# Modulation by weighted sums on VectorE, ScalarE and GpSimd with a matmul of ones, in place of split matmuls

## The chip, the cores and the metric

The kernel runs on one core of a Trainium2 chip. The metric is the device time of one execution in microseconds. One core has five engines with queues of their own that run in order: TensorE (PE in the profile; its weight loads are PEld), VectorE (DVE), ScalarE (ACT), GpSimd (POOL) and SyncE (SP, which issues most DMAs). On-chip memory is SBUF with 128 partitions, and matmuls write to PSUM banks.

## The reference

Two blocks of a small transformer follow each other on 512 tokens x and 256 context tokens ctx, with 1024 features. The first block has two layers (called AB and CD in the kernel). Each is modulated by a conditioning vector, one for x and one for ctx:

```python
mod = silu(c) @ mod_w[l] + mod_b[l]          # [3072], for c of x and of ctx
h, gate = adaln(x, mod)                      # rmsnorm(x) * (1 + scale) + shift
... AB: MLA and GQA attention over [ctx | x];  CD: windowed attention and a short convolution
x = x + gate * (mixed @ w_out)
```

So each layer needs six vectors (shift, scale, gate for x and ctx) of 1024 numbers each, which come out of 2 x 1024 times 1024 x 3072 products. The second block has an even and an odd layer without this modulation.

## The kernel before, in words

All products are made from fp32 operands that are split into a high and a low part in fp32r: `mm3` (lines 236 to 240) issues three matmuls, high x high (L238), high x low (L239) and low x high (L240). `weights` (L210) loads a chunk of weights in pieces of 512 KB into a ring of 3 raw slots (`rawp`), casts each half on ScalarE (L229) and subtracts on VectorE, or in some filler work on GpSimd, for the low part (L232). `split` (L141) does the same for activations (L143, L144). `rstd` (L135) is a root by a power on GpSimd (L138), which each normalisation waits for. Temporaries of up to 2 KB per partition come from `T4`, a ring with the tag `t2` of 5 slots in the stage that the change touches; `sc` holds silu(c) as two columns per feature block, and `sc4` its split.

The modulation of the first layer's shift and scale is made in `start` by `mod_first` and is not touched. The rest comes by chunks of 256 columns. `mod_rows` (L328) loads a chunk, splits it, and multiplies it with `sc4` as the stationary operand of 4 columns: 16 matmuls of 4x256 (L338 for the high part, L339 for the low part) into one F bank, which VectorE copies out as 4 rows (L340), with the bias as a fifth row. `mod_cols` (L343) turns rows into columns by two matmuls with a 5x2 selector (L348). `mods` (L742) does both for eight chunks of layer 1 (the kernel counts layers from 0). For the gates, `gate_rows` (L353) spills the five rows to DRAM and `gate_sum` (L359) loads them again, sums them by a matmul with the selector (L364) and spills two rows.

The tile framework puts the instructions of each engine in an order of its own, worked out by a timeline model from the order in which the code is written, from priorities and from the slots that rings have; engines then wait for each other by semaphores. In `run` (L1424) the AB layer begins with the latents (`ab_lat`, L747: two column chunks, in each three pairs of token tiles, which are projected, normalised, transposed and split), then `mla_proj` for four head groups (`proj(0)` to `proj(3)`), the queries `ab_q` and gates `ab_gates`. `mods` is written in between: chunks 0, 1 between the two halves of `ab_lat`, 2, 3 after it, 4 to 7 between the head groups, and the gate of layer 0 at the end. The first attention scores (L469) follow. In the CD layer, `rest` (L1626) is a generator whose units are spread over the attention items by `pace(items, ru, 21)`; `gate_rows` for layer 1 are four of these units, and `gate_sum` is one.

## Time and profile before

| what | value |
|---|---|
| median of 3 runs | 1550.33 us (1548.44 to 1553.42) |
| profiled execution, first to last instruction | 1546.3 us |
| what lies around it against the median | 4.0 us |
| mean granted TensorE clock | 0.990 of full speed |
| busy: PE, PEld | 96%, 89% of the span |
| busy: DVE, ACT, POOL | 67%, 55%, 35% |
| moved by DMA | 168.2 MB, 109 GB/s in the mean |

The busy shares are means over the whole program. The change touches two stretches: the AB layer's projections, from some 73 us to the first attention score at 254 us, and the CD layer's attention with its fillers, from some 640 to 780 us. What a saved microsecond is worth there has to be read from windows over these stretches, from the waits in them, and from the order of the queues. Matmuls overlap: what one costs is the distance between the starts of two, not the duration of one.

### The profile page before, as it was taken

The page shows a single profiled execution, that of the slowest core. Times are in us where ns is not written, and L with a number is a line of the kernel's source. Part 1 is how long each engine was busy: PE and PEld are TensorE (multiplying, and loading weights), DVE is VectorE, ACT ScalarE, POOL GpSimd, SP SyncE. Part 2 cuts the span into 40 slices and gives each one's busy share as a digit, 9 for nine tenths or more (in the row PEclk, how much of TensorE's full clock was granted, in tenths as well). Part 3 has the DMA queues.
Part 4 walks back from the last instruction along what each step waited for, and adds up shares of the span by engine and source line. Part 5 has one row for each costly group of instructions (what it writes and reads, how often), then busy time and mean ns, then how long its engine had stood idle before and what let it go on. Part 6 is the DMA issues. An engine that isn't in the chain of part 4 may idle for free.

```text
span 1546.3 us, 28606 instructions
## 1 busy us (share of the span) xinstructions
PE 1486.4 (96%) x10760; PEld 1373.0 (89%) x10760; DVE 1036.5 (67%) x2121; ACT 846.5 (55%) x1759; POOL 546.9 (35%) x652
## 2 busy tenths in 40 slices
PE   6899999989999999999999999999999999999998
PEld 3799788877998999888889889998899999998998
DVE  6777887889886477777755458986544465565444
ACT  6545555689996154565643446557433544455322
POOL 1533533567674033232421434444201334443000
PEclk8999999999999999999999999999999999999999
DMA  8344564121221332322234222124334321223423
GB/s 304 121 128 120 183 203 162 45 103 33 63 70 31 146 121 71 101 96 86 93 115 145 80 96 82 66 86 137 116 103 143 119 94 57 82 69 132 148 90 110
DMA packets 60685, 168.20 MB, mean 109 GB/s; under 512 B 9890, under 2 KB 18530, under 8 KB 60546
## 3 DMA queue, kind: packets, MB, share of 16 engines
q1 hardware_dynamic: 54768, 163.52, 31.8%
q10 hardware_dynamic: 5778, 2.84, 0.7%
q8 instruction: 85, 1.39, 0.4%
q14 instruction: 54, 0.44, 0.1%
HBM read 144.06 MB, written 22.28 MB: 108 GB/s over the span
## 4 chain that ended last, share of the span: by engine, by line
PE 79%; DVE 8%; DMA 5%; ACT 3%; issue 2%; POOL 2%; SPq 0%; ACTq 0%; DVEq 0%; POOLq 0%
PE A L240 17%; PE A L238 17%; PE A L239 17%; PE B L524 3%; PE F L238 3%; PE F L239 3%; PE F L240 3%; PE F L595 2%; PE B L238 2%; PE B L239 2%; PE B L240 2%; DVE wl L232 1%; PE B L996 1%; PE B L388 1%; PE B L1168 1%
## 5 line engine op out<-in xcount | busy, mean ns | idle before, releaser
L229 ACT CAST wh<-raw 128x512 fp32r<-128x512 f32 (+1 forms) x388 | 232.4, 616 | 237.8 <-PE A L240 166.9
L232 DVE TENSOR_TENSOR wl<-raw,wh 128x512 fp32r<-128x512 f32 (+1 forms) x320 | 233.4, 744 | 93.9 <-ACT wh L229 90.7
L481 POOL TENSOR_SCALAR P<-P,s 128x768 f32<-128x768 f32 (+3 forms) x192 | 152.8, 801 | 176.4 <-DVE s L1264 33.4
L144 DVE TENSOR_TENSOR PTl<-B,PTh 128x512 fp32r<-128x512 f32 (+2 forms) x208 | 127.9, 633 | 47.7 <-ACT PTh L143 35.0
L232 POOL TENSOR_TENSOR wl<-raw,wh 128x512 fp32r<-128x512 f32 x68 | 90.9, 1338 | 158.3 <-ACT wh L229 132.0
L138 POOL TENSOR_TENSOR s8f<-s8f,mhalf 128x4 f32<-128x4 f32 (+2 forms) x53 | 61.5, 1161 | 227.3 <-DVE s8f L137 119.7
L238 PE MATMUL A<-wh,mh 128*128 128x256 f32 x480 | 136.5, 285 | 2.9 <-ACT mh L143 2.9
L143 ACT CAST PTh<-B 128x512 fp32r<-128x512 f32 (+2 forms) x208 | 108.2, 545 | 53.8 <-PE B L524 27.1
L239 PE MATMUL A<-wl,mh 128*128 128x256 f32 x480 | 136.0, 284 | 0.0
L240 PE MATMUL A<-wh,g 128*128 128x256 f32 x408 | 115.7, 285 | 1.2 <-DVE g L144 1.2
L240 PE MATMUL A<-wh,h2l 128*128 128x256 f32 x384 | 108.7, 286 | 2.5 <-DVE h2l L408 2.5
L238 PE MATMUL A<-wh,h4h 128*128 128x256 f32 x384 | 109.5, 286 | 1.0 <-ACT h4h L407 0.8
L240 PE MATMUL A<-wh,h4l 128*128 128x256 f32 x384 | 108.7, 285 | 0.5 <-DVE h4l L408 0.5
L238 PE MATMUL A<-wh,h2h 128*128 128x256 f32 x384 | 108.9, 284 | 0.3 <-ACT h2h L407 0.3
L239 PE MATMUL A<-wl,h4h 128*128 128x256 f32 x384 | 108.7, 284 | 0.0
L239 PE MATMUL A<-wl,h2h 128*128 128x256 f32 x384 | 108.6, 283 | 0.0
L238 PEld LDWEIGHTS A<-wh,mh 128*128 128x128 f32 x480 | 91.9, 192 | 4.3 <-ACT mh L143 3.3
L239 PEld LDWEIGHTS A<-wl,mh 128*128 128x128 f32 x480 | 92.0, 192 | 0.1
L524 PE MATMUL B<-ident,P 128*128 128x128 f32 x592 | 86.2, 274 | 4.5 <-DVE PTl L144 2.4
L240 PEld LDWEIGHTS A<-wh,g 128*128 128x128 f32 x408 | 78.0, 192 | 1.7 <-DVE g L144 1.7
L490 ACT ACTIVATE P<-A,s 128x768 f32<-128x768 f32 (+1 forms) x96 | 73.2, 766 | 7.4 <-DVE s L488 4.7
L524 PEld LDWEIGHTS B<-ident,P 128*128 128x128 f32 x592 | 67.5, 141 | 9.2 <-POOL P L481 2.5
(515 smaller groups left out, 4914.8 us busy)
## 6 DMA issues: line engine op xcount, KB each, us to landing
raw<-mod_w SPq DMA_DIRECT2D x32, 512.0 KB
raw<-even_w SPq DMA_DIRECT2D x32, 512.0 KB
raw<-odd_w SPq DMA_DIRECT2D x32, 512.0 KB
raw<-cd_w SPq DMA_DIRECT2D x26, 512.0 KB
mraw<-mod_w SPq DMA_DIRECT2D x16, 512.0 KB
raw<-w_ple_gate SPq DMA_DIRECT2D x16, 512.0 KB
raw<-ab_wg SPq DMA_DIRECT2D x8, 512.0 KB
raw<-ab_wo SPq DMA_DIRECT2D x8, 512.0 KB
```

The costliest lines, as they stand in the source:

```text
L138: self.nc.gpsimd.tensor_tensor(out=ms, in0=ms, in1=self.mhalf[:, 0:n], op=ALU.pow)
L143: self.nc.scalar.copy(out=hi, in_=src)
L144: self.nc.vector.tensor_tensor(out=lo, in0=src, in1=f32(hi), op=ALU.subtract)
L229: nc.scalar.copy(out=hi, in_=r)
L232: eng.tensor_tensor(out=lo, in0=r, in1=f32(hi), op=ALU.subtract)
L238: mm(out=out, lhsT=xh, rhs=wh, start=start, stop=False)
L239: mm(out=out, lhsT=xh, rhs=wl, start=False, stop=False)
L240: mm(out=out, lhsT=xl, rhs=wh, start=False, stop=stop)
L481: self.nc.gpsimd.tensor_scalar(out=P, in0=P, scalar1=s, scalar2=0.0, op0=ALU.mult, op1=ALU.add)
L490: nc.scalar.activation(out=P[:, u, :], in_=S[:, u, :], func=AF.Exp, bias=m[:, u:u + 1], scale=1.0, accum_out=s[:, u:u + 1])
L524: nc.tensor.transpose(out=pt[:, j, u, :], in_=b, identity=self.ident)
L595: nc.tensor.matmul(out=O, lhsT=vst(e, j), rhs=pts[j // 2][w][:, j % 2], start=w + j == 0, stop=w == 1 and j == nk - 1)
```

## The change

For the gate of layer 0 (two parts of 512 columns), for shift and scale of layer 1 (four parts) and for the gate of layer 1 (two parts, x alone), the product is no longer made by matmuls over split weights. `acc_part` loads a part by four transfers of 512 KB into the raw ring and goes over the eight feature blocks: VectorE multiplies the raw [128, 512] weights with the column of silu(c) for x and adds to an accumulator `ax`; for ctx, ScalarE multiplies into a temporary of `T4` and GpSimd adds it to an accumulator `ac`. The sum over the 128 partitions is then a matmul in fp32 with a column of ones: `acc_cols` makes 8 of them per part, 128x1 each, for columns; `acc_gate` makes one row of 512 per gate and spills it. The accumulators are halves of gate buffers (`gT[4]` to `gT[7]`), two pairs in turn. The spill of five rows, `mod_rows`, `gate_rows`, `gate_sum` and `mods` go; biases come as inputs of another layout. In CD the counted units become 22 with `pace` still at 21.

```diff
-            self.ab_lat(X, L, latg, lambda: self.mods(0, 1))
-            self.mods(2, 3)
+            gs2 = [[gT[b + i][:, 0:512] for i in range(2)] for b in (4, 6)]
+            am = self.acc_mods([gs2[j] for j in (0, 1, 0, 1, 1, 1)])
...
+            self.ab_lat(X, L, latg, lambda: acc(5))
+            acc(5)
             proj(0)
+            acc(5)
             T["q"] = {0: self.ab_q(X, gp, T, 0)}
+            acc(5)
             proj(1)
-            self.mods(4, 5)
+            acc(5)
             self.ab_gates(X, 2, keep(4))
+            acc(5)
             proj(2)
-            self.mods(6, 7)
             self.ab_gates(X, 3, keep(6))
             proj(3)
-            self.gate_rows(0, range(4))
-            self.gate_sum(0)
             self.ab_gates(X, 0, spill(0))
...
-                    for h in (2 * g, 2 * g + 1):
-                        self.gate_rows(1, (h,))
+                    a3 = self.acc_part(6 + g, (self.tl(cp, [128, 512], "ax", 1), None))
+                    for h in range(2):
+                        next(a3)
+                        next(a3)
                         yield
+                    next(a3, None)
+                    self.acc_gate(1, g)
+                    yield
...
-                self.gate_sum(1)
-                yield
```

The new functions (here and in the rows of the new order below, line numbers are the changed kernel's; `acc(5)` is one whole part):

```python
    def acc_part(self, j, into):
        nc = self.nc
        self.macc = ax, ac = into
        for k in range(8):
            if k % 2 == 0:
                raw = self.tl(self.rawp, [128, 2, 512], "raw")
                nc.sync.dma_start(out=raw, in_=self.I["mod_r"][j][:, k:k + 2, :])
            r = raw[:, k % 2, :]
            if k == 0:
                nc.vector.tensor_scalar(out=ax, in0=r, scalar1=self.sc[:, k, 0:1], scalar2=None, op0=ALU.mult)
            else:
                nc.vector.scalar_tensor_tensor(out=ax, in0=r, scalar=self.sc[:, k, 0:1], in1=ax, op0=ALU.mult, op1=ALU.add)
            if ac is not None:
                if k == 0:
                    nc.scalar.activation(out=ac, in_=r, func=AF.Copy, scale=self.sc[:, k, 1:2])
                else:
                    t = self.T4([128, 512])
                    nc.scalar.activation(out=t, in_=r, func=AF.Copy, scale=self.sc[:, k, 1:2])
                    nc.gpsimd.tensor_tensor(out=ac, in0=ac, in1=t, op=ALU.add)
            if k % 2:
                yield

    def acc_cols(self, j):
        nc = self.nc
        p = self.B()
        for e, a in enumerate(self.macc):
            for b in range(4):
                nc.tensor.matmul(out=p[:, 2 * b + e:2 * b + e + 1], lhsT=a[:, 128 * b:128 * b + 128], rhs=self.ones)
        nc.vector.tensor_tensor(out=self.modT[1][:, 4 * j:4 * j + 4, :], in0=p[:, 0:8].rearrange("p (b e) -> p b e", e=2),
                                in1=self.mbias[:, 4 * j:4 * j + 4].unsqueeze(2).to_broadcast([128, 4, 2]), op=ALU.add)

    def acc_gate(self, layer, h, bank="F"):
        nc = self.nc
        for e, a in enumerate(self.macc):
            if a is not None:
                cs = slice(512 * h, 512 * h + 512)
                r, p = self.T4([1, 512]), self.B(bank)
                nc.scalar.dma_start(out=r, in_=self.I["mod_bg"][layer:layer + 1, cs])
                nc.tensor.matmul(out=p[0:1, :], lhsT=self.ones, rhs=a)
                nc.vector.tensor_tensor(out=r, in0=p[0:1, :], in1=r, op=ALU.add)
                nc.sync.dma_start(out=self.gsum_d[layer][e:e + 1, cs], in_=r)
```

**First place: GpSimd's queue at the latents.** The code of `ab_lat` before and in the change; L138, now L143, is the power of a normalisation (`s_...`), and each pair of token tiles of the latents has one of 128x2. Before:

```order
L138 TENSOR_TENSOR s_238_1039<-s_238_1039,mhalf 128x2
L138 TENSOR_TENSOR s_243_1105<-s_243_1105,mhalf 128x2
L138 TENSOR_TENSOR s_248_1171<-s_248_1171,mhalf 128x2
L138 TENSOR_TENSOR s_289_1345<-s_289_1345,mhalf 128x2
L138 TENSOR_TENSOR s_294_1411<-s_294_1411,mhalf 128x2
L138 TENSOR_TENSOR s_299_1477<-s_299_1477,mhalf 128x2
L138 TENSOR_TENSOR s8f_1599<-s8f_1599,mhalf 128x4
```

Now:

```order
L143 TENSOR_TENSOR s_238_1042<-s_238_1042,mhalf 128x2
L143 TENSOR_TENSOR s_243_1108<-s_243_1108,mhalf 128x2
L363 TENSOR_TENSOR g_20_116<-g_20_116,t_251_1192 128x512
L143 TENSOR_TENSOR s_248_1174<-s_248_1174,mhalf 128x2
L363 TENSOR_TENSOR g_20_116<-g_20_116,t_253_1198 128x512
L363 TENSOR_TENSOR g_20_116<-g_20_116,t_254_1202 128x512
L363 TENSOR_TENSOR g_20_116<-g_20_116,t_256_1208 128x512
L363 TENSOR_TENSOR g_20_116<-g_20_116,t_257_1212 128x512
L363 TENSOR_TENSOR g_20_116<-g_20_116,t_259_1218 128x512
L363 TENSOR_TENSOR g_20_116<-g_20_116,t_260_1222 128x512
L143 TENSOR_TENSOR s_278_1310<-s_278_1310,mhalf 128x2
L143 TENSOR_TENSOR s_283_1376<-s_283_1376,mhalf 128x2
```

Behind the second pair's power, the first part's seven additions into `g_20` stand around the third pair's power (`s_248`) and ahead of those of the second chunk.

**Second place: ScalarE's queue at the same point.** L755, now L782, squares a pair of latents, L143, now L148, casts the transposed latents, and L229, now L234, casts weights. Before, with the modulation's weights `wh` among the latents' work, up to the first cast for the next chunk that follows there:

```order
L229 CAST wh_1274<-raw_1272 128x512
L229 CAST wh_1278<-raw_1272 128x512
L229 CAST wh_1284<-raw_1282 128x512
L279 COPY t_246_1167<-A_1118 128x512
L229 CAST wh_1288<-raw_1282 128x512
L143 CAST lTh_949<-B_1045 128x2x256
L755 ACTIVATE t_247_1169<-t_246_1167 128x512
L333 DMA t_260_1204<-mod_b 1x256
L143 CAST lTh_949<-B_1111 128x2x256
L333 DMA t_273_1248<-mod_b 1x256
L143 CAST lTh_949<-B_1177 128x2x256
L229 CAST wh_1492<-raw_1490 128x512
```

Now:

```order
L148 CAST lTh_952<-B_1048 128x2x256
L782 ACTIVATE t_247_1172<-t_246_1170 128x512
L362 ACTIVATE t_251_1192<-raw_1187,sc 128x512
L362 ACTIVATE t_253_1198<-raw_1195,sc 128x512
L148 CAST lTh_952<-B_1114 128x2x256
L362 ACTIVATE t_254_1202<-raw_1195,sc 128x512
L362 ACTIVATE t_256_1208<-raw_1205,sc 128x512
L362 ACTIVATE t_257_1212<-raw_1205,sc 128x512
L362 ACTIVATE t_259_1218<-raw_1215,sc 128x512
L148 CAST lTh_952<-B_1180 128x2x256
L362 ACTIVATE t_260_1222<-raw_1215,sc 128x512
L234 CAST wh_1239<-raw_1237 128x512
```

Where casts of modulation weights stood, the scaled copies (L362) stand, each into a temporary `t_...` that an addition on GpSimd frees; behind them stands `wh_1239`, the first cast of the second chunk of latent weights.

**Third place: TensorE's queue in the head projections.** F is the bank of the modulation's columns, B those of the head projections. Before, the end of a modulation chunk:

```order
L238 MATMUL A_2275<-hTh_122,wh_2216 128x512
L239 MATMUL A_2275<-hTl_123,wh_2216 128x512
L240 MATMUL A_2275<-hTh_122,wl_2217 128x512
L348 MATMUL F_2152<-sel_79,t_435_2132 128x2 x2
L238 MATMUL B_2029<-whf_2025,lTh_949 128x256
L239 MATMUL B_2029<-wlf_2026,lTh_949 128x256
L240 MATMUL B_2029<-whf_2025,lTl_950 128x256
```

Now, where shift and scale's second part ends (L373 are the matmuls with ones):

```order
L243 MATMUL B_2459<-whf_2367,lTh_952 128x384
L244 MATMUL B_2459<-wlf_2368,lTh_952 128x384
L245 MATMUL B_2459<-whf_2367,lTl_953 128x384
L373 MATMUL F_2034<-ones,g_22_118 128x1 x4
L243 MATMUL B_2483<-whf_2363,lTh_952 128x384
L244 MATMUL B_2483<-wlf_2364,lTh_952 128x384
L245 MATMUL B_2483<-whf_2363,lTl_953 128x384
```

The matmuls with ones of `g_22`, the accumulator for ctx, stand in the middle of the projections of `proj(2)`. On GpSimd, the seven additions into that accumulator are ordered like this now, from the second to the last (`mk_2044`, L877, are the keys of `proj(1)`, and `s8f` normalisations):

```order
L363 TENSOR_TENSOR g_22_118<-g_22_118,t_401_2007 128x512
L363 TENSOR_TENSOR g_22_118<-g_22_118,t_402_2011 128x512
L143 TENSOR_TENSOR s8f_2096<-s8f_2096,mhalf 128x4
L877 TENSOR_TENSOR mk_2044<-t2f_2065,mgk_959 128x4x64
L363 TENSOR_TENSOR g_22_118<-g_22_118,t_404_2017 128x512
L877 TENSOR_TENSOR mk_2044<-t2f_2092,mgk_959 128x4x64
L363 TENSOR_TENSOR g_22_118<-g_22_118,t_405_2021 128x512
L143 TENSOR_TENSOR s8f_2123<-s8f_2123,mhalf 128x4
L363 TENSOR_TENSOR g_22_118<-g_22_118,t_407_2027 128x512
L877 TENSOR_TENSOR mk_2044<-t2f_2119,mgk_959 128x4x64
L143 TENSOR_TENSOR s8f_2382<-s8f_2382,mhalf 128x4
L363 TENSOR_TENSOR g_22_118<-g_22_118,t_408_2031 128x512
```

The additions alternate with the powers and key products of `proj(1)`, and the accumulator is whole only with the last of these rows, behind three key products and three powers.

## Rows read from the trace of the kernel before

**Rows 1.** Page, span and busy time of each engine.

```profile
span 1546.3 us, 28606 instructions
...
PE 1486.4 (96%) x10760; PEld 1373.0 (89%) x10760; DVE 1036.5 (67%) x2121; ACT 846.5 (55%) x1759; POOL 546.9 (35%) x652
```

**Rows 2.** Windows (start:end, wall; busy PE, PEld, DVE, ACT, POOL; clock; DMA; GB/s).

```profile
100.00:240.00 140.00, 136.54 (x955) 120.51 (x954) 110.27 (x259) 75.51 (x152) 52.10 (x49) 1.00 0.54 172
640.00:780.00 140.00, 139.68 (x820) 118.40 (x819) 103.87 (x238) 88.21 (x200) 44.30 (x69) 1.00 0.27 88
```

**Rows 3.** Waits of PE, 60 to 255 us (the longest: total, times, longest).

```profile
PE A L240 <- DVE wl L232: 1.5, 1, 1.5
```

**Rows 4.** Waits of PE, 640 to 780 us (the only one).

```profile
PE F L238 <- DVE t2f L340: 0.3, 1, 0.3
```

**Rows 5.** Instructions of line L338 (duration min/median/max, first and last start).

```profile
L338 PE MATMUL F<-wh,sc x128: 275/276/362, 73.7 to 732.3; 128*4 128x256 f32 x128
```

**Rows 6.** Timeline of PE (start us, us, instruction) in the AB layer's projections.

```profile
103.27 0.60 PE L348 MATMUL F<-sel,t 5*128 5x2 f32 x4
103.80 0.39 PE L239 MATMUL A<-wl,hTh 128*128 128x256 f32 x1
...
106.61 0.28 PE L339 MATMUL F<-wl,sc 128*4 128x256 f32 x1
...
108.24 0.28 PE L339 MATMUL F<-wl,sc 128*4 128x256 f32 x1
...
235.72 1.01 PE L364 MATMUL F<-t,sel 5*2 5x512 f32 x2
```

**Rows 7.** Groups by form, 60 to 255 us (busy us, mean ns | idle before, releaser).

```profile
L232 DVE TENSOR_TENSOR wl<-raw,wh 128x512 fp32r<-128x512 f32 x76 | 53.2, 724 | 4.7 <-ACT wh L229 4.6
...
L229 ACT CAST wh<-raw 128x512 fp32r<-128x512 f32 x76 | 44.1, 619 | 26.6 <-PE F L338 6.7 <-DMA raw<-mod_w 5.1 <-DMA raw<-ab_wg 4.6
...
L138 POOL TENSOR_TENSOR s8f<-s8f,mhalf 128x4 f32<-128x4 f32 x24 | 27.9, 1165 | 40.2 <-DVE s8f L137 39.9
...
L850 POOL TENSOR_TENSOR mk<-t2f,mgk 128x256 f32<-128x256 f32 x12 | 10.1, 839 | 12.2 <-DVE t2f L848 6.5 <-DMA qkv_d<-mk 5.7
...
L138 POOL TENSOR_TENSOR s<-s,mhalf 128x2 f32<-128x2 f32 x6 | 5.5, 913 | 26.5 <-DVE s L137 26.4
...
L163 DVE SCALAR_TENSOR_TENSOR g<-t,A 128x512 f32<-128x512 f32 x4 | 2.7, 674 | 0.0
```

**Rows 8.** Page, group of GpSimd's subtractions.

```profile
L232 POOL TENSOR_TENSOR wl<-raw,wh 128x512 fp32r<-128x512 f32 x68 | 90.9, 1338 | 158.3 <-ACT wh L229 132.0
```

**Rows 9.** Timeline of POOL, two products of 128x512.

```profile
152.55 1.54 POOL L191 TENSOR_TENSOR t<-t,TQ 128x512 f32<-128x512 f32 x1
...
164.33 1.66 POOL L191 TENSOR_TENSOR t<-t,TQ 128x512 f32<-128x512 f32 x1
```

**Rows 10.** Timeline of DVE at the same times.

```profile
152.85 1.78 DVE L193 TENSOR_TENSOR q<-t,TQ 128x512 f32<-128x512 f32 x1
...
164.15 0.69 DVE L193 TENSOR_TENSOR q<-t,TQ 128x512 f32<-128x512 f32 x1
```

**Rows 11.** Timeline of SP, the two issues of a chunk's loads.

```profile
110.75 9.58 SPq L222 DMA_DIRECT2D raw<-ab_wq  x2
```

**Rows 12.** Timeline of ACT, the cast that waits for the second of these loads.

```profile
123.77 1.14 ACT L229 CAST wh<-raw 128x512 fp32r<-128x512 f32 x2 [0.58 <-DMA raw<-ab_wq]
```

**Rows 13.** Timeline of PE, the matmuls behind a pause.

```profile
76.58 0.39 PE L238 MATMUL A<-wh,hTh 128*128 128x256 f32 x1 [1.35 <-ACT pk L702]
...
80.21 0.41 PE L238 MATMUL A<-wh,hTh 128*128 128x256 f32 x1
```

**Rows 14.** Timeline of PE, end of the first latent chunk; first attention score.

```profile
97.56 0.28 PE L240 MATMUL A<-wh,hTl 128*128 128x256 f32 x1
...
254.49 0.36 PE L469 MATMUL A<-kA,qs 128*128 128x256 f32 x1 [0.92 <-DVE t L163]
```

More of the change, by code (lines that the diff above doesn't have):

```diff
@@ L108, in setup @@
         self.dram = ent(self.pool("dram", space=DRAM))
-        self.grow_d, self.gsum_d = ([self.dram.tile([n, 1024], F32, name=f"g{n}row{l}_d") for l in range(2)] for n in (5, 2))
+        self.gsum_d = [self.dram.tile([2, 1024], F32, name=f"grow{l}_d") for l in range(2)]
         self.rot_d = [self.dram.tile([128, 4, 2, n], F32, name=f"rot{n}_d") for n in (16, 32)]
@@ L115, in setup @@
         nc.vector.memset(self.mhalf, -0.5)
+        self.ones = c.tile([128, 1], F32, name="ones")
+        nc.vector.memset(self.ones, 1.0)
         self.sel2 = c.tile([5, 2], F32, name="sel2")
@@ L121, in setup @@
         nc.scalar.dma_start(out=self.ng, in_=I["norm_g_2"])
+        self.mbias = c.tile([128, 16], F32, name="mbias")
+        nc.scalar.dma_start(out=self.mbias, in_=I["mod_bc"])
+        nc.vector.tensor_scalar(out=self.mbias[:, 8:16], in0=self.mbias[:, 8:16], scalar1=1.0, scalar2=None, op0=ALU.add)
         self.modT = [c.tile([128, 16, 2], F32, name=f"modT{l}") for l in range(2)]
@@ L326, in mod_first @@
         return rows, self.sel2
-    def mod_rows(self, layer, ch):
-        nc = self.nc
-        W = self.weights(self.I["mod_w"][layer, ch])
-        rows = self.T4([5, 256])
-        nc.scalar.dma_start(out=rows[4:5, :], in_=self.I["mod_b"][layer:layer + 1, 256 * ch:256 * ch + 256])
-        p = self.B()
-        for k0, hi, lo in W:
-            for k in range(hi.shape[1]):
-                kk = k0 + k
-                nc.tensor.matmul(out=p[0:4, 0:256], lhsT=self.sc4[:, kk, :], rhs=hi[:, k, :], start=kk == 0, stop=False)
-                nc.tensor.matmul(out=p[0:4, 0:256], lhsT=self.sc4[:, kk, :], rhs=lo[:, k, :], start=False, stop=kk == 7)
-        nc.vector.tensor_copy(out=rows[0:4, :], in_=p[0:4, 0:256])
-        return rows, self.sel2
     def mod_cols(self, layer, ch, rs):
@@ L351, in mod_cols @@
                                      op0=ALU.mult, op1=ALU.add)
-    def gate_rows(self, layer, chs):
-        for h in chs:
-            rows, _ = self.mod_rows(layer, 8 + h)
-            self.nc.sync.dma_start(out=self.grow_d[layer][:, 256 * h:256 * h + 256], in_=rows)
-    def gate_sum(self, layer, bank="F"):
-        for h in (0, 512):
-            rows, r, p = self.T4([5, 512]), self.T4([2, 512]), self.B(bank)
-            self.nc.sync.dma_start(out=rows, in_=self.grow_d[layer][:, h:h + 512])
-            self.nc.tensor.matmul(out=p[0:2, :], lhsT=self.sel2, rhs=rows)
-            self.nc.scalar.copy(out=r, in_=p[0:2, :])
-            self.nc.sync.dma_start(out=self.gsum_d[layer][:, h:h + 512], in_=r)
+    def acc_part(self, j, into):
+        nc = self.nc
+        self.macc = ax, ac = into
+        for k in range(8):
+            if k % 2 == 0:
[4 more added lines that the diff above has]
+                nc.vector.tensor_scalar(out=ax, in0=r, scalar1=self.sc[:, k, 0:1], scalar2=None, op0=ALU.mult)
+            else:
+                nc.vector.scalar_tensor_tensor(out=ax, in0=r, scalar=self.sc[:, k, 0:1], in1=ax, op0=ALU.mult, op1=ALU.add)
+            if ac is not None:
+                if k == 0:
+                    nc.scalar.activation(out=ac, in_=r, func=AF.Copy, scale=self.sc[:, k, 1:2])
+                else:
+                    t = self.T4([128, 512])
[3 more added lines that the diff above has]
+                yield
@@ L368, in gate_bc, with acc_mods @@
+    def acc_mods(self, slots):
+        for j in range(6):
+            yield from self.acc_part(j, slots[j])
+            if j < 2:
+                self.acc_gate(0, j)
+            else:
+                self.acc_cols(j - 2)
+            yield
     def gate_bc(self, layer, out, which=0):
@@ L740, in ab_q @@
         return q
-    def mods(self, *chs):
-        for ch in chs:
-            self.mod_cols(1, ch, self.mod_rows(1, ch))
     def ab_lat(self, X, L, latg, between):
```

13 lines of the change are left out of this document (12 added, 1 removed).

## The prediction

> **What bounds the kernel now.** I read the page first: TensorE is busy for 1486.4 of 1546.3 us, VectorE for 67% [rows 1]. That is a mean over many stages, so the next view is the windows over the two stretches that the change touches [rows 2]: TensorE has 136.5 of 140 us in the AB layer's projections and 139.7 of 140 in the CD layer's attention, at full clock in both, with VectorE at 110.3 and 103.9. Then the waits of TensorE in the same stretches: the longest in AB is 1.5 us, for VectorE's subtraction [rows 3], and in CD there is one, of 0.3 us [rows 4]. So in both stretches TensorE sets the pace, and a microsecond taken from its queue is worth a microsecond, as long as nothing new makes it wait. The other engines have slack in the mean, and the question is whether their queues still serve TensorE in time.
>
> **What TensorE loses and gains.** The distance between starts counts, not the 276 ns duration. Between 106.61 and 108.24 us there are 14 matmuls of 4x256 [rows 6], hence 0.1164 us each. Of the 256 of them (128 per line [rows 5]; L339 has as many), 192 are in AB and 64 in CD: 22.4 and 7.4 us. The column matmuls take 0.53 us for four records [rows 6], 0.133 each, and 32 records are in AB: 4.3 us. The row sums take 1.01 us for two records, 0.505 each, with four per layer: 2.0 us each. Removed: 28.7 in AB, 9.4 in CD.
>
> Added in AB: 32 matmuls with ones, at two records per fp32 matmul (the selector's two matmuls show four) 64 x 0.133 = 8.5 us. No row has a matmul of one output column; the nearest is this 128x2 one. Each now loads 128 columns of weights anew, so from 0.1 us a record (6.4) to 0.25 (16) is possible; I take the row. Gate rows: four matmuls of 512 columns, eight records x 0.505 = 4.0. In CD two of them: 2.0. Net on TensorE: AB 12.5 - 28.7 = **-16.2 us**, CD 2.0 - 9.4 = **-7.4 us**.
>
> **The other engines.** On VectorE 48 subtractions of 0.724 in AB become 48 multiply-adds; the scalar form of that shape took 0.674 [rows 7]: 2.4 us less, and the small copies out of PSUM about balance. CD is one for one. ScalarE's 48 casts in AB (0.619 us [rows 7]) become 48 scaled copies, taken at the same price, and in CD 16 casts (9.9 us) go. GpSimd gets 42 additions of 128x512. The nearest row is its subtraction of two operands at 1.338 us [rows 8]; 42 x 1.338 = 56 us onto the 52.1 that it is busy for in the AB window [rows 2]. Per part it is 7 x 1.338 = 9.4 us in one chain. The mean still fits: some 108 of 140. The weights that are loaded keep their bytes, and a part's four loads use the raw ring as two old chunks did. Loads, casts, adds and copies all lie beside TensorE in the mean, so none of them is in the sum by itself; what is, is where TensorE now waits for their chain.
>
> **New waits in AB.** Two things change in the queues. A normalisation's power (0.91 us for 128x2, 1.165 for 128x4 [rows 7]) now stands behind additions on GpSimd; and ScalarE's copies need a temporary that such an addition must free, while weight casts for TensorE stand behind them on ScalarE. I walked along the new order of the five queues with these prices from the end of the first latent chunk (97.56 us [rows 14]; 95.6 in the new order, 16 matmuls less) to the first score (254.49). By the walk TensorE waits six times:
> - **7.6 us** at the start of the second latent chunk. Its first weights need a raw slot that part 0 frees. ScalarE gets to part 0's copies at 96.7; two copies, a cast and a copy (4 x 0.62) must pass, then the load: the second of two issues, at 120.0, landed at 123.7 [rows 11, 12], so 3.7 us; then the cast (0.62): 103.5, and 1 us more for temporaries that wait for additions. TensorE was ready at 96.9.
> - **4.6 us** in the second latent chunk, at the transposes of a pair whose power stands behind part 1's first addition, and **3.1 us** for the PSUM bank that this pair frees late.
> - **1.2 us** at the queries' weights.
> - **11.1 us** at the matmuls with ones of part 3. From its second to its last addition stand 6 x 1.338 + 3 x 1.165 + 3 x 0.839 = 14 us of GpSimd, 16 with the first; the copies can start at about 170, TensorE is there at 176 for the x columns (3.4, by VectorE's chain) and at 179 for those of ctx, which are whole at 187 (7.7). Behind them stand head projections that need nothing of them.
> - **2.5 us** at part 5, whose last load waits for a slot.
>
> Together **+30.1 us**. They aren't fully new: 256-column matmuls at 0.1164 each (others by their columns, small ones at the prices above) sum to 131 us between the two points in the new order, while the old stretch less removed plus added work is 156.9 + 1.9 - 28.7 + 12.5 = 142.6. So 11.3 us of today's small pauses lie in it. Some will fall together with the new ones; I take half, **-5.6 us** (ends: 0 and -11.3). After a pause the matmuls can run slower: behind a wait of 1.35 us at 76.58, the matmul at 80.21 still took 0.41 instead of 0.28 us [rows 13]. Some 3.6 us at 0.28 / 0.41 of the pace lose 1.2 us; I count nothing for it in the sum, and for five pauses up to 6 us in the range.
>
> **The sum.** 1546.3 - 16.2 + 30.1 - 5.6 in AB, and -7.0 in CD (of the 7.4; TensorE never waits there [rows 4], the additions are VectorE's alone, and there is no new GpSimd work; ends 0 and -8.4): 1547.6 us for the span. The profiled execution lies 4.0 us below the median, so **1551.5 us**. About 0.3%, 4.7 us, is what a measurement of this kernel can tell from no change; the forecast is no measurable change, and both layers are: AB about 8 slower, CD 7 faster.
>
> **A row against a rule.** Beside GpSimd's product of 128x512 at 152.55 (1.54 us [rows 9]), VectorE's product that started 0.30 us after it took 1.78 us, and the same product that started 0.18 us ahead of one took 0.69 [rows 10]; GpSimd's then took 1.66. So an addition on GpSimd can cost VectorE up to 1.09 us, and the loss falls on whichever starts second. In the sum I count nothing for it, as VectorE has 30 us of slack in the window [rows 2]. The Trainium skill (SBUF — State Buffer, "SBUF: two separate sides") states that VectorE with two SBUF inputs and GpSimd reading SBUF share a port pair as an exclusive lock: whoever starts first holds it for a whole instruction. By that rule every one of the 42 additions could block VectorE for its length; the trace agrees in the one pair of rows (1.78 against 0.69), and the rule speaks against this change. What that gives is the second rival.
>
> **Rivals.**
> *1. TensorE's saving comes through.* If copies run ahead (the first additions start before the latents' powers are due, or cost 1.0 us instead of 1.34), the waits shrink. With none: 1546.3 - 16.2 - 7.4 + 4.0 = **1526.7 us**; with half of them, 15 us, and half of the old pauses gone (-2.8), about **1539**. For it: mean load fits on every engine. Against: the powers and the additions stand in one queue, written into the order, and the raw ring has 3 slots.
> *2. Slower: VectorE becomes the bound in AB through GpSimd's additions.* Its busy time in the window is 110.3 - 2.4 = 108 of 140 us. Every addition that catches a two-operand instruction costs up to 1.09 us: 42 x 1.09 = 46, hence 154 us. VectorE runs at 0.79 of the window now; I allow it 0.9 before TensorE waits for it throughout. In the forecast's stretch of 148 us that is 133, so it decides from 25 us on, 0.6 us per addition. At 0.8 us (34 us in all) the stretch becomes 142 / 0.9 = 158, 10 us over the forecast: about **1561 us**; at the full price 154 / 0.9 = 171, 23 over: **1575**. For it: the pair of rows. Against: VectorE's work on PSUM operands isn't such a pair, and only additions that lie on such an instruction count.
> *3. CD gains nothing,* because the 22nd unit runs behind the attention or VectorE's 16 multiply-adds come late: 1551.5 + 7 = **1558**.
> *4. The change does not do what it says:* the products with ones need whole accumulators, so fewer matmuls but the same time; that is the forecast itself.
>
> **Chances.** Forecast (1547 to 1555) 0.36; rival 1 in whole or part (below 1546) 0.32, the whole of it 0.07; rivals 2 and 3 (above 1555) 0.32, of it 0.20 for the second. Faster by over 0.3%: 0.32, within: 0.36, slower: 0.32. The range of 8 in 10 leaves out the whole of rival 1 and the upper half of rival 2: from 1533 to 1567. The forecast's own range is 1544 to 1559 (the old pauses' two ends, and a third of the 6 us of slow matmuls).
>
> **What the profile would show.** Right: no 4x256 matmuls outside the start, TensorE's busy time near 24 us less and its share below 96%; additions of about 1.3 us on GpSimd; TensorE waiting in the latents for ScalarE's first cast and for a transposed pair's power, and some 8 to 11 us at the matmuls with ones for GpSimd's accumulator; the first score at 260 to 265 us, and CD 7 us shorter. Wrong: TensorE's waits before the first score below 15 us in total (rival 1), or waits of TensorE for VectorE's subtractions throughout the stage, with VectorE's multiply-adds well over 0.7 us in the mean (rival 2). The sum falls if an addition costs under 1 us or the matmul with one column over 0.25 us a record.

## The result and the profile after

The changed kernel takes 1601.8 us (median of 4 runs, 1599.18 to 1603.39) against 1549.5 us for the kernel before: a ratio of 1.0335, 95% interval 1.0314 to 1.0357. It is slower by 52 us, outside the predicted range (1533 to 1567) and far above the forecast of no change (1551.5).

The page of the changed kernel, span and busy times, and the granted clock in 40 slices:

```profile
span 1599.2 us, 28125 instructions
...
PE 1491.1 (93%) x10540; PEld 1376.8 (86%) x10540; DVE 1077.5 (67%) x2109; ACT 840.7 (53%) x1739; POOL 607.8 (38%) x694
...
PEclk8988869999999999999999999999999999999999
```

TensorE has 220 matmuls fewer than before and is busy 5 us *longer* [rows 1]: part of its work ran at a lower clock. That is in the slices from the third to the sixth, the AB layer's projections. The windows of the changed kernel there and over the whole stretch to the attention (columns as in [rows 2]):

```profile
100.00:240.00 140.00, 104.29 (x570) 90.88 (x571) 120.87 (x196) 61.63 (x112) 92.48 (x72) 0.77 0.42 137
60.00:300.00 240.00, 190.81 (x1142) 170.74 (x1140) 186.69 (x339) 106.42 (x203) 136.55 (x118) 0.84 0.40 128
```

Against [rows 2], TensorE is busy 104 instead of 137 of 140 us, at 0.77 of the clock instead of 1.00; VectorE does fewer instructions (196 against 259) in more time (121 against 110 us); GpSimd goes from 52 to 92. The first attention score (the timeline of TensorE; before, 254.49 [rows 14]) has moved by 50 us, to 304.25:

```profile
304.25 0.28 PE L501 MATMUL A<-kA,qs 128*128 128x256 f32 x1
```

That is nearly the whole loss; from there to the end the changed kernel needs 1294.9 us against 1291.8. What TensorE waits for from 60 to 305 us (total, times, longest; the largest entries):

```profile
PE B L793 <- DVE t L788: 11.7, 3, 5.6
PE F L373 <- POOL g L363: 6.3, 3, 2.4
PE F L373 <- DVE g L356: 5.5, 3, 2.5
PE B L243 <- ACT t2f L852: 4.9, 2, 3.6
PE B L243 <- ACT t2f L284: 4.9, 3, 3.0
PE A L243 <- DVE g L168: 4.2, 2, 3.2
```

Where before the longest wait was 1.5 us [rows 3], there are waits at the latents' transposes (L793), at the matmuls with ones (L373) for both accumulators, and at the head projections for banks that ScalarE empties late (L852, L284). All waits of TensorE from 60 us to the first score sum to 49.1 us, before to 8.6.

**How one wait comes about.** At the third pair of latents, the timelines of GpSimd and VectorE:

```profile
96.87 1.26 POOL L363 TENSOR_TENSOR g<-g,t 128x512 f32<-128x512 f32 x1 [3.07 <-ACT t L362]
98.24 0.70 POOL L143 TENSOR_TENSOR s<-s,mhalf 128x2 f32<-128x2 f32 x1
98.92 9.12 POOL L363 TENSOR_TENSOR g<-g,t 128x512 f32<-128x512 f32 x6
```

```profile
97.01 1.15 DVE L142 TENSOR_SCALAR s<-s 128x2 f32<-128x2 f32 x1
98.08 0.68 DVE L149 TENSOR_TENSOR lTl<-B,lTh 128x512 fp32r<-128x512 f32 x1
98.98 2.90 DVE L788 SCALAR_TENSOR_TENSOR t<-t,s,latg 128x256 f32<-128x256 f32 x2 [0.23 <-POOL s L143]
101.80 3.43 DVE L356 SCALAR_TENSOR_TENSOR g<-raw,sc,g 128x512 f32<-128x512 f32 x2
```

An instruction on 128x2 (L142), which takes 0.17 us where GpSimd does not add, took 1.15 beside an addition that had started 0.14 us ahead of it; the two that normalise the pair took 2.90 (0.88 for the pair before it); two multiply-adds took 3.43 instead of 1.54. L149, which reads PSUM, took its usual 0.68. Six more additions run one after another on GpSimd from 98.92 us on. TensorE stands at the transposes of that pair:

```profile
100.61 0.45 PE L793 MATMUL B<-ident,t 128*128 128x128 f32 x1 [5.19 <-DVE t L788]
101.93 0.90 PE L793 MATMUL B<-ident,t 128*128 128x128 f32 x3 [0.87 <-DVE t L788]
105.28 1.01 PE L385 MATMUL F<-g,ones 128*1 128x512 f32 x1 [2.45 <-DVE g L356]
```

The Trainium skill (SBUF — State Buffer, "SBUF: two separate sides") states that VectorE, in a 2-port mode or with two SBUF inputs, and GpSimd share a port pair as an exclusive lock for a whole instruction. The trace agrees for the two-operand forms (L788, L356), and L142 was held up as well (1.15 against 0.17), though it has one SBUF operand; whether it runs in a 2-port mode no trace shows.

Only a part of the 5.19 us is such a hold-up. In TensorE's new order nothing stands between the last projection of that pair, which starts at 94.27 us, and its transposes; before, matmuls of the next chunk and of the modulation stood there, and the transposes came at 105.81 us, 8.2 us behind the last projection [rows 14], without a wait. In e2, a run without any addition, the same wait is still 3.27 us (the timelines of TensorE, before and e2):

```profile
105.81 0.27 PE L766 MATMUL B<-ident,t 128*128 128x128 f32 x1
```

```profile
98.60 1.21 PE L792 MATMUL B<-ident,t 128*128 128x128 f32 x4 [3.27 <-ACT t L362]
```

So more than half of this wait is the bare chain of a normalisation (copy, square, sum, power, product) that TensorE now has no other work to cover.

**How a queue makes another.** At 203 us, the timeline of ScalarE, and then TensorE's:

```profile
203.72 0.72 ACT L362 ACTIVATE t<-raw,sc 128x512 f32<-128x512 f32 x1 [1.26 <-POOL g L363]
204.35 0.46 ACT L852 COPY t2f<-B 128x384 f32<-128x384 f32 x1
```

```profile
204.86 0.69 PE L243 MATMUL B<-whf,lTh 128*128 128x384 f32 x1 [3.61 <-ACT t2f L852]
```

A scaled copy waits for a temporary that an addition frees; the copy that empties TensorE's bank stands behind it on ScalarE; TensorE waits 3.61 us for that bank.

**What follows a pause.** After TensorE had waited 2.15 us, the first of its matmuls and one 4 us later (timeline), and the window between them with its granted clock:

```profile
153.41 0.58 PE L244 MATMUL A<-wl,hTh 128*128 128x256 f32 x1 [2.15 <-DVE wl L237]
...
157.63 0.41 PE L243 MATMUL A<-wh,hTh 128*128 128x256 f32 x1
```

```profile
154.00:158.00 4.00, 4.00 (x20) 4.00 (x20) 1.86 (x4) 2.15 (x5) 3.92 (x4) 0.50 0.70 201
```

The clock was granted at half, 1.2 of 2.4 GHz, the 256-column matmul starts 0.21 us apart instead of 0.117. The longest such stretch is from 190 to 223 us (window):

```profile
190.00:223.00 33.00, 21.09 (x65) 18.01 (x66) 30.53 (x49) 17.99 (x33) 27.89 (x23) 0.50 0.63 208
```

From 60 us to the first score the distances between the starts of matmuls, without the waits, sum to 32 us more than at full pace (the median distance of each width before; for the matmuls with ones their own at full clock); before, to 7 us.

So the AB layer's balance is: TensorE's work -16, waits +41 (49.1 - 8.6), slow matmuls +25: +50, against 49.8 measured.

**The CD layer.** Only multiply-adds on VectorE were added there. The waits of TensorE from 640 to 840 us:

```profile
PE F L243 <- DVE cc L1047: 3.0, 1, 3.0
PE F L243 <- ACT cc L1044: 1.5, 1, 1.5
PE B L1023 <- ACT PTh L148: 0.6, 1, 0.6
```

All waits there sum to 6.1 us; before, in the same work 50 us earlier (590 to 790 us), to 1.1. A block of the convolution (`cc`) comes late from VectorE, whose multiply-adds stand in front of it and wait for their weights (VectorE's timeline, then the block):

```profile
698.55 0.75 DVE L356 SCALAR_TENSOR_TENSOR ax<-raw,sc,ax 128x512 f32<-128x512 f32 x1 [0.86 <-DMA raw<-mod_r]
...
699.30 0.67 DVE L1047 TENSOR_TENSOR cc<-F,cc 128x512 f32<-128x512 f32 x1
```

The clock behind it is not full (0.96 from 680 to 720 us). The distance between the two kernels is 51 us before the CD layer and 52 at its last scores: no gain.

### The profile page after: what moved, and what is told of

It is laid out like the page before. It is cut to its first block, busy times and chain, and to the rows that moved or that the text cites. A ratio compares the mean times of both kernels' runs of the same rounds, so it can differ in the third digit from the quotient of the medians.

```text
span 1599.2 us, 28125 instructions
## 1 busy us (share of the span) xinstructions
PE 1491.1 (93%) x10540; PEld 1376.8 (86%) x10540; DVE 1077.5 (67%) x2109; ACT 840.7 (53%) x1739; POOL 607.8 (38%) x694
## 4 chain that ended last, share of the span: by engine, by line
PE 71%; DVE 9%; DMA 4%; ACT 4%; issue 4%; POOL 4%; ACTq 0%; DVEq 0%; POOLq 0%; SPq 0%
PE A L243 16%; PE A L245 15%; PE A L244 15%; PE B L556 3%; PE F L243 3%; PE F L244 3%; PE F L245 3%; PE F L627 2%; DMA raw<-mod_r 2%; DVE wl L237 1%; PE B L243 1%; PE B L244 1%; PE B L245 1%; PE B L1023 1%; POOL s8f L143 1%
## 5 line engine op out<-in xcount | busy, mean ns | idle before, releaser
L234 ACT CAST wh<-raw 128x512 fp32r<-128x512 f32 (+1 forms) x324 | 195.3, 615 | 221.9 <-PE A L245 163.7
L237 DVE TENSOR_TENSOR wl<-raw,wh 128x512 fp32r<-128x512 f32 (+1 forms) x256 | 191.7, 760 | 92.7 <-ACT wh L234 90.1
L149 DVE TENSOR_TENSOR PTl<-B,PTh 128x512 fp32r<-128x512 f32 (+2 forms) x208 | 128.1, 633 | 43.6 <-ACT PTh L148 37.7
L143 POOL TENSOR_TENSOR s8f<-s8f,mhalf 128x4 f32<-128x4 f32 (+2 forms) x53 | 61.9, 1168 | 233.9 <-DVE s8f L142 221.8
L148 ACT CAST PTh<-B 128x512 fp32r<-128x512 f32 (+2 forms) x208 | 108.6, 545 | 50.2 <-PE B L556 22.3
L520 DVE TENSOR_REDUCE s<-A 128x1 f32<-128x768 f32 (+1 forms) x80 | 71.7, 896 | 7.9 <-PE A L502 5.6
```

The costliest lines, as they stand in the source:

```text
L143: self.nc.gpsimd.tensor_tensor(out=ms, in0=ms, in1=self.mhalf[:, 0:n], op=ALU.pow)
L148: self.nc.scalar.copy(out=hi, in_=src)
L149: self.nc.vector.tensor_tensor(out=lo, in0=src, in1=f32(hi), op=ALU.subtract)
L234: nc.scalar.copy(out=hi, in_=r)
L237: eng.tensor_tensor(out=lo, in0=r, in1=f32(hi), op=ALU.subtract)
L520: nc.vector.tensor_reduce(out=m, in_=S, axis=AX.X, op=ALU.max, negate=True)
```

## The experiments

Two theories at first. A: the additions hold up VectorE's instructions. B: GpSimd's queue as such (powers and temporaries behind 42 instructions). Rivals: C, VectorE's multiply-adds and ScalarE's copies; D, VectorE's load.

One thing holds for e1, e2, e3, e5, e6, e9 and e10: with each edit the framework orders the queues anew, so a difference is that of the edit together with its new order. In e1 TensorE's order differs from that of the changed kernel from the 547th matmul on and GpSimd's from the 59th instruction, though the expectation says that it stays; in the other six, 70 to 120 more matmuls stand ahead of the first score than in the changed kernel. Only e12 has its order up to there. A run with the same edits and TensorE's order held fixed was not made, so what the order by itself costs stays open.

**e1, a short-operand instruction in place of each addition.**

```diff
-                    nc.gpsimd.tensor_tensor(out=ac, in0=ac, in1=t, op=ALU.add)
+                    nc.gpsimd.tensor_tensor(out=ac[:, 0:8], in0=self.base8, in1=t[:, 0:8], op=ALU.pow)
```

> Each of the 42 additions of 128x512 on GpSimd is replaced by a power of 128x8, which reads and writes 8 columns instead of 512 and takes about 1.6 us against 1.55 us; ScalarE's copies, the temporaries, the accumulators' waits and GpSimd's order stay as in the changed kernel (the output for ctx is not the reference's). Theory A, additions on GpSimd hold up VectorE's instructions: VectorE's multiply-adds fall from 0.93 to about 0.75 us in the mean, and the time falls to 1555 to 1575 us. Theory B, what costs is the queue alone (powers and temporaries behind 42 instructions of 1.5 us): the time stays at 1590 to 1605 us.

Measured 1589.65 us (ratio to before 1.025, 1.0219 to 1.0281). The groups of e1 and of the changed kernel (busy, mean ns; GpSimd's instruction, VectorE's multiply-add):

```profile
L365 POOL TENSOR_TENSOR g<-base,t 128x8 f32<-128x8 f32 x42 | 73.6, 1755 | 10.9 <-ACT t L364 9.9
L358 DVE SCALAR_TENSOR_TENSOR g<-raw,sc,g 128x512 f32<-128x512 f32 x41 | 31.2, 761 | 15.2 <-DMA raw<-mod_r 14.8
```

```profile
L363 POOL TENSOR_TENSOR g<-g,t 128x512 f32<-128x512 f32 x42 | 65.0, 1550 | 10.1 <-ACT t L362 8.5 <-ACT g L359 0.4
L356 DVE SCALAR_TENSOR_TENSOR g<-raw,sc,g 128x512 f32<-128x512 f32 x41 | 38.1, 929 | 4.9 <-DMA raw<-mod_r 4.6
```

VectorE's multiply-adds became 0.17 us shorter as theory A expected, and its busy time from 100 to 240 us fell from 121 to 96. Yet only 12 of the 52 us went, although GpSimd's instruction is 0.2 us longer, which B would charge. So VectorE's lateness is real and costs some 12 us (a little more if the longer instruction cost something); most of the loss is elsewhere. Theory A alone has fallen.

**e2, the additions left out.**

```diff
-                    nc.gpsimd.tensor_tensor(out=ac, in0=ac, in1=t, op=ALU.add)
```

> The 42 additions on GpSimd are left out, so the ctx sums lack seven of eight terms; ScalarE's copies into the temporaries stay. Theories A and B alike: 1530 to 1550 us, since both make GpSimd's additions the cause. Theory C, VectorE's 48 multiply-adds and ScalarE's 48 copies in front of the latents and head projections cost most: above 1575 us.

Measured 1570.46 us (1.0126, 1.01 to 1.0153): 31 us less than the changed kernel, 19 less than e1. That is what 42 long instructions in GpSimd's queue cost, temporaries and accumulators that wait for them included. But 20 us above before remain with no addition at all, so neither theory was whole, and C has a part.

**e3, the ctx sums on VectorE.**

```diff
-                    nc.scalar.activation(out=ac, in_=r, func=AF.Copy, scale=self.sc[:, k, 1:2])
+                    nc.vector.tensor_scalar(out=ac, in0=r, scalar1=self.sc[:, k, 1:2], scalar2=None, op0=ALU.mult)
...
-                    t = self.T4([128, 512])
-                    nc.scalar.activation(out=t, in_=r, func=AF.Copy, scale=self.sc[:, k, 1:2])
-                    nc.gpsimd.tensor_tensor(out=ac, in0=ac, in1=t, op=ALU.add)
+                    nc.vector.scalar_tensor_tensor(out=ac, in0=r, scalar=self.sc[:, k, 1:2], in1=ac, op0=ALU.mult, op1=ALU.add)
```

> The ctx sums are made on VectorE too, by 48 more instructions of 0.74 us (35 us), without ScalarE's copies, temporaries and GpSimd's additions. If GpSimd's additions are the cause (A or B): 1540 to 1560 us. Theory D, VectorE's load is the bound, wherever it comes from: VectorE would need 143 of 140 us in the stretch, and the time stays at 1575 us or more.

Measured 1571.29 us (1.012, 1.0094 to 1.0146): between the two expectations. Without GpSimd and without copies the largest loss is one place, on TensorE's timeline:

```profile
187.40 0.80 PE L243 MATMUL A<-hTh,wh 128*128 128x512 f32 x1 [14.15 <-ACT wh L234]
```

It waits for the gates' weights. SyncE's timeline has their load at 183 us:

```profile
183.00 4.19 SPq L227 DMA_DIRECT2D raw<-ab_wg  x2
```

That load needs a slot of the raw ring, whose slots before it in the order go to weights that VectorE had yet to go through. That the slot is what it waited for is read from the order, not from a run.

**e5, a quarter of the loads and products.**

```diff
         for k in range(8):
+            if ac is not None and k > 1:
+                if k % 2:
+                    yield
+                continue
```

> In the AB layer each part keeps one of its four loads and two of its eight products (12 multiply-adds, 12 copies, 6 additions left); the matmuls with ones all stay (the sums lack six of eight terms). If TensorE's saving was priced rightly and only the accumulation's cost hid it: the 16 us of AB come on top of what the run with CD alone gained, 1523 to 1532 us. If the plan itself (matmuls with ones in the middle of projections, a different order of the queues) costs: 1545 us or more.

Measured 1532.25 us (0.9873, 0.9837 to 0.9909), at the upper end of the first expectation. The window of e5 in the stretch:

```profile
100.00:240.00 140.00, 136.88 (x940) 125.65 (x939) 106.55 (x241) 68.99 (x141) 60.25 (x58) 0.99 0.40 136
```

TensorE is full again, at full clock, and the first score comes at 242.3 us, 12 us ahead of before, although 72 matmuls more stand ahead of it than in the changed kernel. The last 5000 matmuls are the same, in the same order, in before and e5; they start 20 us earlier in e5 (853.0 against 873.3 us), where -16.2 for AB and -7.4 for CD were predicted. So the matmuls with ones and TensorE's saving were priced about rightly; the loss is the accumulation, with the order that it brings.

**e6, the sums for x alone.**

```diff
-            if ac is not None:
+            if ac is not None and k == 0:
                 if k == 0:
```

> As the run without additions, and ScalarE's 42 scaled copies into temporaries are left out too; VectorE's 48 multiply-adds for x and all 24 loads through the raw ring stay. Theory C1, loads that hold the three raw slots and VectorE waiting for them: the time stays within 8 us of the 1570 us measured without additions. Theory C2, ScalarE's copies in front of the weight casts: it falls to 1530 to 1545 us.

Measured 1555.65 us (1.0032, 1.0011 to 1.0053): 15 us below e2, which is ScalarE's copies, and 23 us above e5. Between the two expectations again.

**e9 and e10, loads without VectorE's time, and VectorE's time without loads.** From e6:

```diff
+                w = 512 if ac is None else 16
-                nc.vector.scalar_tensor_tensor(out=ax, in0=r, scalar=self.sc[:, k, 0:1], in1=ax, op0=ALU.mult, op1=ALU.add)
+                nc.vector.scalar_tensor_tensor(out=ax[:, 0:w], in0=r[:, 0:w], scalar=self.sc[:, k, 0:1], in1=ax[:, 0:w], op0=ALU.mult, op1=ALU.add)
```

> From the run with x alone (1555.7 us): all 24 loads of AB and their slots stay, but the 42 multiply-adds on VectorE work on 16 of 512 columns (about 0.1 us each instead of 0.76, so 28 us of VectorE's time go; sums incomplete). Theory L, loads, raw slots and the order of the queues cost the 23 us between the run with x alone and the one with a quarter of the loads: 1550 to 1556 us. Theory V, VectorE's time costs them: 1532 to 1538 us.

```diff
-            if k % 2 == 0:
+            if k % 2 == 0 and (k == 0 or ac is None):
```

> The mirror image: all multiply-adds for x at full width, but each part of AB has one load instead of four, whose two halves are used four times (18 loads of 512 KB fewer; sums of the wrong blocks). Theory L: 1532 to 1540 us. Theory V: 1550 to 1556 us.

Measured 1540.27 (0.9939, 0.9919 to 0.996) and 1543.58 us (0.9963, 0.9942 to 0.9983): 8 and 11 us above e5, of the 23 that both together cost. Neither theory holds alone: the two make 19 of the 23. That a late VectorE holds slots, and that slots held make the next loads late, is how I read the rest; no run shows it.

Put in a row, the medians make a ladder, each step with the order that the framework made for it: 1532 with a quarter, +23 for the loads and VectorE's multiply-adds, +15 for ScalarE's copies, +19 for GpSimd's queue, +12 for what its additions do to VectorE: 1602.

**e8, another place for layer 1's shift and scale.**

```diff
+        def mods():
+            for j in range(4):
+                into = tuple(self.tl(box["ga"], [128, 512], x, 1) for x in ("max", "mac"))
+                yield from self.acc_part(2 + j, into)
+                self.acc_cols(j)
...
+        mu = mods()
+        self.pace(late, mu, 17)
```

> CD as in the changed kernel; in AB the gate of layer 0 as before, and layer 1's shift and scale by multiply-adds on VectorE for x and ctx alike (64 of 0.74 us, no GpSimd, no temporaries), spread over the attention of three head groups instead of the projections. TensorE loses 19 us in the projections and gets 8.5 us in the attention, where it has some 20 us of idle time: 1527 to 1535 us. If VectorE's 47 us more delay the attention's softmax there: 1541 to 1560 us.

Measured 1568.43 us (1.0098, 1.0074 to 1.0123). The first score comes 20 us earlier than before (234.1 us), and from there to the end e8 needs 42 us more. TensorE's longest entry in the attention is a wait for probabilities, 10.5 us in 13 times; that VectorE's new instructions stand in front of the softmax is my reading of it. The idle time of TensorE was not free room.

**e4, e7 and e12: the CD layer by itself.** e4 is the kernel before with CD's part of the change; in e7 that part is traced behind the gated blocks; e12 has the new AB and the old CD.

```diff
 # e4
-                    for h in (2 * g, 2 * g + 1):
-                        self.gate_rows(1, (h,))
+                    a3 = self.acc_part(6 + g, (self.tl(cp, [128, 512], "ax", 1), None))
...
 # e7, against e4
-                    a3 = self.acc_part(6 + g, (self.tl(cp, [128, 512], "ax", 1), None))
...
                 for g in range(2):
                     for b, p, _, _ in self.feat(Xx, self.weights(I["cd_w"][11 + g])):
...
+                    a3 = self.acc_part(6 + g, (self.tl(cp, [128, 512], "ax", 1), None))
...
 # e12, against the changed kernel
-                    a3 = self.acc_part(6 + g, (self.tl(cp, [128, 512], "ax", 1), None))
+                    for h in (2 * g, 2 * g + 1):
+                        self.gate_rows(1, (h,))
```

> AB as in the kernel before, CD as in the changed one (gate of the CD layer by multiply-adds on VectorE and matmuls with ones). By TensorE's saving alone 7.4 us faster than before: 1542 us. If VectorE's multiply-adds delay the convolution's blocks as in the changed kernel, where TensorE waited 3.0 us for one and then ran slowly: within 3 us of before, 1547 to 1552 us.

> CD alone, with the gate's parts traced behind the gated blocks instead of between the convolution's halves. If VectorE's waits for a part's loads hold up the convolution (TensorE waited 3.3 us for it with CD alone): 1536 to 1539 us. If they only move to what comes behind: 1540 to 1544 us.

> AB as in the changed kernel, with the same order of all queues there, and CD as before. If what CD alone gained (9 to 10 us) is there beside the new AB too: 1609 to 1613 us. If it is not, as the comparison of the two traces behind the first attention suggests (the delay of 50 us does not shrink in CD): 1598 to 1604 us.

Measured 1541.18 us (0.994, 0.9924 to 0.9957), 1542.24 (0.995, 0.9929 to 0.997) and 1596.53 (1.0311, 1.0286 to 1.0337). CD alone looks like the gain that I had priced, and e12, below both of its ranges, says that the same part gains nothing in the changed kernel. In e7 TensorE's wait for the convolution's block is 1.3 us instead of 3.3 in e4, and the time is the same. In e4's trace TensorE still waits 3.3 us for the convolution's block, and no gain lies between the start and the end of the CD layer. So something else had to make e4 faster.

**e13 to e17: what else e4 brought.** It has two more inputs and a constant cell of ones. e13 is the kernel before with both and nothing moved; e14 has the cell alone, e15 the inputs alone; e16 has no cell and no new instruction, but one column more in a neighbouring constant; e17 a cell of 16 columns.

```diff
 # e14 (e17: [128, 16])
+        self.ones = c.tile([128, 1], F32, name="ones")
+        nc.vector.memset(self.ones, 1.0)
 # e15
+    d["mod_r"] = chunks(np.concatenate([g["mod_w"][0][:, 2048:], g["mod_w"][1]], 1), 512)
+    d["mod_bg"] = A(g["mod_b"][:, 2048:3072])
 # e16
-        self.mhalf = c.tile([128, 16], F32, name="mhalf")
+        self.mhalf = c.tile([128, 17], F32, name="mhalf")
```

> The kernel before with nothing moved: only the additional inputs in their new layout (read by nothing) and the memory cell of ones, set at the start; every queue has the same order as before. If the 9 to 10 us that CD alone gained come from CD's part of the change: 1549 to 1553 us. If they come from something outside the code of CD (where tensors lie, the start): 1540 to 1545 us.

> The kernel before with the cell of ones and its setting alone, no new inputs. If where tensors lie in the device's DRAM makes the 7 us of the run with both: 1549 to 1553 us. If the cell (4 bytes per partition that move what lies behind it in SBUF, and one instruction more on VectorE at the start) makes them: 1542 to 1546 us.

> The kernel before with the two new inputs alone, which nothing reads, and no cell of ones. The mirror image: 1542 to 1546 us if the place of tensors in DRAM makes the 7 us, 1549 to 1553 us if the cell does.

> The kernel before with one more column (4 bytes per partition) in the constant beside which the cell of ones would stand, and no instruction more. If the cell's place in SBUF (what lies behind it moves) makes the 8 us: 1540 to 1546 us. If the additional instruction on VectorE does: 1548 to 1553 us.

> The kernel before with a cell of 16 ones (64 bytes per partition) instead of one. If any additional instruction at the start, or any shift, makes the 8 us: 1540 to 1546 us. If only a shift by few bytes does: 1548 to 1553 us.

Measured 1543.66 us for e13 (0.9955, 0.9941 to 0.997), 1541.68 for e14 (0.9944, 0.9925 to 0.9964), 1549.48 for e15 (0.9998, 0.9983 to 1.0013), 1542.52 for e16 (0.9953, 0.9937 to 0.9969) and 1545.36 for e17 (0.9964, 0.9951 to 0.9976). The inputs do nothing; a few bytes more among the constants in SBUF, with or without an instruction, make 5 to 8 us. Against e14 (1541.7) or e13 (1543.7), CD's part (e4, 1541.2) is worth nothing measurable: the intervals overlap.

**e11, a search for a better version:** CD as in e4, and the gate of layer 0 spread over the MLA attention in its old form.

```diff
-            self.gate_rows(0, range(4))
-            self.gate_sum(0)
...
+        self.pace(late, gate0(), 5)
```

> Search for a better version: as with CD alone (1541 us), and the gate of layer 0 in its old form (64 matmuls of 4x256 and the row sums, 9.5 us of TensorE) is spread over the MLA attention instead of standing in the projections. TensorE has some 20 us of idle time there: 1532 to 1538 us. If it is put into the way of the attention (one F bank that its outputs use too): 1541 to 1550 us.

Measured 1547.95 us (0.9981, 0.9965 to 0.9996), worse than e4. The fastest that compute the reference are e4 and e14 at 1541 to 1542 us, and they owe it to the cell.

## Why the prediction was wrong

- **What bounds the kernel:** right. TensorE was full in both stretches, and with the accumulation cut to a quarter (e5) the first score came 12 us earlier and the last 5000 matmuls 20, against 16.2 predicted for AB and 23.6 for both layers.
- **The price of TensorE's work:** about right. The records of the matmuls with ones start 0.11 us apart at full clock, 0.21 at half, and 0.13 in the median, as put.
- **"Together +30.1 us"**, less 5.6 for today's pauses: this is the first step that failed. The sum was +41, not +24.5. At the latents the figures came near, but that was in part luck. 7.6 us were put at the second chunk's first weights, behind ScalarE's copies and a raw slot; no such wait came. The 8.5 us measured up to 105 us are at the transposes of the first chunk's third pair (5.19 and 0.87) and at VectorE's accumulator (2.45). 4.6 us were put at the second chunk's transposes, and 5.63 measured; of these 3.64 remain without additions (e2). Three things were missing. The walk had each instruction of VectorE at its undisturbed price; it did not see that a normalisation's chain lies bare where no other matmul stands ahead of its transposes; and apart from one bank at the latents it looked at TensorE's waits for accumulators and weights, while head projections waited for banks behind scaled copies (3.05, 3.61 us). At part 3's matmuls with ones, where it put 11.1 us, the waits were 2.5 and 2.2 us: TensorE came there later, after the waits at the head projections.
- **"I count nothing for it in the sum"**, of additions that hold up VectorE: the second failure. VectorE was busy 25 us longer from 100 to 240 us than in e1, with fewer instructions; 33 of the 42 additions lie there, hence 0.75 us per addition, above the 0.6 that the rival named as its threshold. Its multiply-adds took 0.93 us in the mean, the sign named for rival 2. By e1 this was worth 12 us of the total. Rival 2 had the sign and the mechanism, but took it for a cause of its own, where it came on top of the queue.
- **"I count nothing for it in the sum, and for five pauses up to 6 us"**, of slow matmuls: the third. 25 us more than before: there were 18 pauses of over 1 us, not five, behind a pause of 2.15 us 21 matmuls ran at half clock, and from 190 to 223 us all did.
- **"In CD -7.0"**: failed. New waits gave back what TensorE saved: from the first score to the last 5000 matmuls TensorE waits 29.4 us in the changed kernel and 23.2 in e12, which has the old CD, and the stretch takes 619.9 and 619.2 us. e4's gain was the cell's. "TensorE never waits there" was a row of the kernel before, and the change put VectorE's wait for loads in front of the block that TensorE waits for: rival 3, which I had put at 1558 by itself.
- **Beside the sum:** three terms of opposite sign cancelled in the forecast. Each of the failures went the same way. I read them as one chain, in which a late VectorE keeps slots, the slots keep loads, the loads keep casts, and slow matmuls follow the pauses; no run shows that chain as a whole.

That slow matmuls make 25 of the 50 us is read from the trace; a run that keeps TensorE busy in the pauses was not made. The changed kernel, which has the cell and one more constant, shows none of the cell's gain in its trace: its last 5000 matmuls, the same in the same order in all these kernels, take 675.0 us to the end of the span, and 672.2 in e12 with the same constants; before they take 673.0, in e15 675.2, in e14 669.1 and in e16 669.3 (one trace each).

## What to carry to other kernels

When TensorE is full and work is moved off it, price the new chain by its latency in each queue that it passes, not by the busy time that it adds: here every engine had room in the mean, and the sums in four queues cost 70 us over a version with a quarter of the loads and products. Look at the slots that a chain holds (raw weights, temporaries, banks) and at what stands behind the instruction that waits for one. When a part of a change is tried alone, try also the parts that do nothing, such as a constant: here that was all of the gain.

## What the runs showed of the hardware

A few bytes more in a constant in SBUF, which presumably shift the tiles behind it, change this kernel by 0.4 to 0.6%: with one column more in a constant (e16) TensorE's order and the instruction count are those of before, and TensorE's busy time is shorter; its waits do not shrink (56.1 us in all in e16, 54.5 before). The page of e16, beside [rows 1]:

```profile
span 1541.0 us, 28606 instructions
...
PE 1479.5 (96%) x10760; PEld 1364.5 (89%) x10760; DVE 1036.7 (67%) x2121; ACT 846.0 (55%) x1759; POOL 551.2 (36%) x652
```

The gain lies spread over the program: e13's trace is 1.0 us ahead of before at the first score, 1.7 at 1000 us, 4.1 at the end. It is in the pace of the matmuls: among the last 5000, some 3760 matmuls of 256 columns that follow one another without a wait start 120.8 ns apart in the mean before and in the changed kernel, 119.4 in e14 and 119.5 in e16, which makes about 5 us. Not each change of place helps: the changed kernel has the cell and one more constant, and not this pace. Why a place matters was not settled. An effect of this size (0.4 to 0.6%) is more than the 0.3% that the prediction took for the limit of what can be told: comparisons between kernels with different constants carry it.

Additions of 128x512 on GpSimd also lengthened VectorE's smallest instructions in SBUF (0.17 to 1.15 us), not only those with two large operands, while those that read PSUM kept their time.
